# The state-space projection as seven products of tile sums, run between gate tiles that are moved there

## The chip, the core and the metric

The kernel runs on one core of a Trainium2 chip. A core has a matrix engine (TensorE, PE in the profile), VectorE (DVE), ScalarE (ACT), GpSimd (POOL) and SyncE (SP), which issues most of the weight loads. Each engine works through a queue of its own in order and waits on semaphores of the others. The metric is the device time of one execution in microseconds; the median of three runs before the change is 2598.36 (2598.11 to 2598.48).

## What is computed

One layer of a hybrid encoder over 384 tokens (256 of a prompt and 8 x 16 of running streams), all in float32. Cut to what matters:

```
proj = rmsnorm(x) @ w_in                      # pool | z | xBC | dt | gates, gates = 2 x 2048 columns
a_pool = pool_mixer(proj_pool)                # 384 x 2048
a_ssd  = gated_rmsnorm(ssd_scan(...), z)      # 384 x 4096
br_pool = a_pool @ w_pool_proj                # 2048 x 2048
br_ssd  = a_ssd  @ w_ssd_proj                 # 4096 x 2048   <- the state-space projection
merged = sigmoid(gate_A) * br_pool + sigmoid(gate_B) * br_ssd
x = x + rmsnorm(merged @ w_out)               # 2048 x 2048
x = x + rmsnorm(relu(rmsnorm(x) @ w_up)**2 @ w_down)
```

## The kernel before

Activations lie transposed in SBUF, channels on the 128 partitions and the 384 tokens along the row. To keep float32 precision at the speed of the float32r form, each operand is split in a high part (ACT copies it to float32r: `wh`, `xgh`) and a low part (DVE takes the difference: `wl`, `xgl`), and each product is three matmuls: high by high, high by low, low by high. A weight tile of 128 x 1024 (512 KB) is loaded by SP (`wfetch`), split by one ACT and one DVE instruction (`wsplit`) into pools of three buffers each, and then used by 24 matmuls of 384 columns (`half`) or, where tokens are stationary and the weights move, by 18 matmuls of 512 columns (`moving`).

The stages, in order of time in the profiled execution:

- up to 585 us: the norm, the pooling branch and its projection. `gate_a(i)` makes tile i of the first gate (product with `w_ga`, times `rstd`, sigmoid), `pool_out(i)` multiplies it with the pool product and stores it in DRAM as `ma_scr[i]`. All sixteen of them are made here, the last twelve in blocks of four ahead of the four `pool_out` that use them.
- to about 1150: the scan over eight groups; its result goes to DRAM as `a_scr[0..31]`, one tile of 128 channels each. Between and behind its last steps come the tiles of the second gate (`gate_b(i)`, stored as `gb_scr[i]`), 0 to 7. A list `queue` of weight loads runs three splits ahead of their use (`take`). The scan's last norm (`finish`, `store`) stands at 1184 on DVE, beside gate tiles 8 to 15, and POOL stores the four last `a_scr` tiles behind it.
- 1246 to 1496: the state-space projection, `pj_sp`: 16 output tiles, each 32 channel tiles x 3 matmuls of 384 columns, weights stationary. Behind each tile DVE multiplies with `gbr` (loaded from `gb_scr`), adds `mar` (loaded from `ma_scr`), and ACT and DVE split the sum into `mh` and `ml`, the left operands of the next product. `gbr` and `mar` have two buffers each and are loaded by POOL.
- to about 1620: the product with `w_out`, tokens stationary: four column blocks of 512, each eight weight tiles (units) of two channel tiles, into three PSUM banks, one for each block of 128 tokens.
- to 2596: the MLP. Its down projection already uses the scheme that the change brings to the state-space projection, and its names are the same: for token blocks 0 and 1, two halves of the channels and two column blocks of 512, the 2 x 2 block product is made with seven products of sums in place of eight (`b11, b21, U, b22, W, V, X`), four more make block 2 as before. Sums of the token tiles (slots 6 to 9 of ten) are made by DVE, sums of the weights by one load with addition on POOL (`accum_op`) and by three DVE additions (`AHEAD`). A product `m` has a PSUM bank that is filled from the accumulator `acc` by an ACT copy (a seed, `opened`) and copied back by ACT or added by DVE (`taken`). `converted` turns the nine accumulators into the six output blocks. The forms run as two behind each half tile of the up projection.

The order on each engine comes from a list scheduler, which places instructions by the order of the program and by when it takes them to be ready; the hardware then runs each queue as placed. PSUM has two banks for projections (`mmtile`) and six others (`sstile`).

Of the kernel before, what the change touches and what calls it, by code (L numbers as in the profile page):

```python
# [14 lines left out]
P = 128  # L15
# [18 lines left out]
def build(ctx, tc, io):  # L34
# [110 lines left out]
    def moving(o, units, lhs, tail, done, pool=None, own=0, hook=None, mid=None, held=None):  # L145
# [12 lines left out]
        for kp in range(n - tail):  # L158
            wh, wl = take(*units[kp])
            with behind(last[0] if chain[0] else None):  # L160
                for k2 in range(2):
                    for b in range(3):
                        mm(b, wh, wl, kp * 2 + k2, k2)
            if hook and kp in hook:
                hook[kp]()
        w = [wload(*units[kp]) for kp in range(n - tail, n - own)]
# [46 lines left out]
    a_scr = [dram.tile([P, T], F32, name=f"a_scr{i}") for i in range(32)]  # L213
    ma_scr = [dram.tile([P, T], F32, name=f"ma_scr{i}") for i in range(KD)]
# [15 lines left out]
    yx = small.tile([P, 56], F32, name="yx")[:, :3]  # L230
# [137 lines left out]
    tok = small.tile([P, 11, NH], F32, name="tok")  # L368
    decb = small.tile([P, NH, NB], F32, name="decb")
    with tc.tile_pool(name="phc", bufs=1, reuse_waits="tile") as pc, tc.tile_pool(name="phc2", bufs=2, reuse_waits="tile") as pc2:  # L370
# [94 lines left out]
        def pool_out(i, sg):  # L465
            ps = proj([io["w_pp"][i, q] for q in range(2)], A, f"pp{i}")
            v.tensor_tensor(halves(sg), even_odd(ps), halves(sg), ALU.mult)
            gp.dma_start(ma_scr[i], sg)
# [98 lines left out]
        for nb in range(4):  # L567
            if nb:
                sg = [gate_a(nb * 4 + i) for i in range(4)]
            for i in range(4):  # L570
                pool_out(nb * 4 + i, sg[i])
            if nb == 0:
                dt_turn(srcs)

    def gate_b(i, pool, tag, hook=None):
        ps = proj([io["w_gb"][i, q] for q in range(2)], xg, f"gb{i}", hook)
        t = pool.tile([P, T], F32, tag=tag, name=f"gbt{i}")
# [5 lines left out]
    with tc.tile_pool(name="phd", bufs=2, reuse_waits="tile") as pd, tc.tile_pool(  # L583
# [350 lines left out]
        queue.extend((io["w_gb"][i, q], f"gb{i}_{q}") for i in range(KD) for q in range(2))  # L934
        queue.extend((io["w_ssd"][i, q], f"sp{i}_{q}") for i in range(KD) for q in range(4))
        queue.extend((io["w_out"][nb, kp], f"wo{nb}_{kp}") for nb in range(4) for kp in range(8 if nb < 3 else 3))
# [146 lines left out]

    mpool = ExitStack()
    with ExitStack() as phe:
        pe1 = phe.enter_context(tc.tile_pool(name="phe", bufs=1, reuse_waits="tile"))
        pe2 = phe.enter_context(tc.tile_pool(name="phe2", bufs=4, reuse_waits="tile"))
        pe4 = phe.enter_context(tc.tile_pool(name="phe4", bufs=2, reuse_waits="tile"))
        ab = []

        def aload():
            for i in (len(ab), len(ab) + 1):
                a = pe2.tile([P, T], F32, tag="ar", name=f"ar{i}")
                sy.dma_start(a, a_scr[i])
                h = pe1.tile([P, T], F32R, name=f"abh{i}")
                l = pe1.tile([P, T], F32R, name=f"abl{i}")
                with later():
                    s.activation(h, a, AF.Copy)
                    v.tensor_tensor(l, a, h.bitcast(F32), ALU.subtract)
                ab.append((h, l))  # L1100

        for i in range(8, KD):
            gate_b(i, pe4, "gbt", aload)
        chain[0] = False
        main.close()
        mp = mpool.enter_context(tc.tile_pool(name="mp", bufs=1, side="right", reuse_waits="tile"))
        for i in range(KD):
            ma, gb = (mp.tile([P, T], F32, tag=f"{n}r", name=f"{n}r{i}", bufs=2) for n in ("ma", "gb"))
            gp.dma_start(ma, ma_scr[i])
            gp.dma_start(gb, gb_scr[i])  # L1110
            ps = proj([io["w_ssd"][i, q] for q in range(4)], ab, f"sp{i}")
            h = mp.tile([P, T], F32R, name=f"mh{i}")
            l = mp.tile([P, T], F32R, name=f"ml{i}")
            v.tensor_tensor(halves(gb), even_odd(ps), halves(gb), ALU.mult)
            v.tensor_tensor(ma, ma, gb, ALU.add)
            s.activation(h, ma, AF.Copy)
            v.tensor_tensor(l, ma, h.bitcast(F32), ALU.subtract)
            ms_.append((h, l))

    res = ctx.enter_context(tc.tile_pool(name="res", bufs=1, reuse_waits="tile"))  # L1120

    r2 = res.tile([P, T], F32, name="r2")
# [24 lines left out]
    for b in range(3):  # L1147
        sy.dma_start(x1[:, b, :], io["x_tok"][b])
    NE = 4
    upool = ExitStack()  # L1150
    pg0 = upool.enter_context(tc.tile_pool(name="pg0", bufs=1, reuse_waits="tile"))
# [7 lines left out]
    xtiles(pg0, NE)  # L1159
    with tc.tile_pool(name="phf", bufs=1, side="right", reuse_waits="tile") as pf, tc.tile_pool(  # L1160
# [80 lines left out]
        for nb in range(4):  # L1241
# [3 lines left out]
            o = [sstile(f"wo{nb}_{b}") for b in range(3)]  # L1245
# [4 lines left out]
            def done(b):  # L1250
# [22 lines left out]
                [(io["w_out"][nb, kp], f"wo{nb}_{kp}") for kp in range(8)],  # L1273
# [6 lines left out]
                {(2, 3): first_turns} if nb == 3 else None,  # L1280
            )
# [125 lines left out]
    with tc.tile_pool(name="phg", bufs=1, side="right", reuse_waits="tile") as pg, tc.tile_pool(  # L1407
# [3 lines left out]
        ORDER = ("b11", "b21", "U", "b22", "W", "V", "X")  # L1411
        AHEAD = {
            "U": ("W", "U", "U", "b22", ALU.add),
            "b22": ("V", "b11", "W", "b11", ALU.subtract),
            "W": ("X", "b21", "b21", "W", ALU.add),
        }
        USES = {
            "b11": ((0, 0), (7, 2)),
            "b21": ((1, 3), (7, 5)),
            "b22": ((2, 8), (8, 9)),  # L1420
            "X": ((3, 4),),
            "U": ((4, 6),),
            "W": ((5, 7),),
            "V": ((6, 1), (8, 2)),
        }
        SEEDED = (0, 1, 2, 3, 4, 5, 6)
        LEFT = {(0, 0): 1, (0, 1): 2, (1, 0): 3, (1, 1): 6, (2, 0): 7, (2, 1): 8}
        first = {m: f for f in reversed(ORDER) for m, _ in USES[f]}
        final = {m: f for f in ORDER for m, _ in USES[f]}
# [3 lines left out]
        def ff_tile(f8, ps, plain):  # L1433
# [16 lines left out]
            elif q:  # L1450
                x = V2[p]
                for o, a, b in ((6, 1, 4), (7, 0, 6), (8, 3, 7), (9, 5, 2), (1, 1, 0)):
                    v.tensor_tensor(x[:, o], x[:, a], x[:, b], ALU.subtract)
# [4 lines left out]
        hacc = lambda b, nb: acc[:, nb // 2 * 9 + LEFT[b, nb % 2], :]  # L1458

        def split(w, name):  # L1460
            h = wpool.tile([P, 1024], F32R, tag="wh", name=f"wh_{name}")
            l = wpool.tile([P, 1024], F32R, tag="wl", name=f"wl_{name}")
            s.activation(h, w, AF.Copy)
            v.tensor_tensor(l, w, h.bitcast(F32), ALU.subtract)
            return h, l

        def quad(G4, np_):
            c8, g = divmod(G4, 2)
            fh, fl = FH[g], FL[g]
            bank, kept = {}, {}  # L1470

            def load():
                for i, j in ((1, 2), (1, 1), (2, 1), (2, 2)):
                    w = pg.tile([P, 1024], F32, tag="wd", name=f"w_b{i}{j}_{G4}_{np_}", bufs=7)
                    sy.dma_start(w, io["w_down"][c8, np_ * 2 + j - 1, g * 2 + i - 1])
# [279 lines left out]
```

## Time and profile before

| what | number |
|---|---|
| median of three runs | 2598.36 us |
| profiled execution, its time | 2597.85 us |
| its span from first to last instruction | 2596.0 us |
| TensorE clock granted, mean | 0.999 |
| `pj_sp` stage | 1246.3 to 1495.7 us |
| `pj_ga` matmuls, all sixteen tiles | 768, 326 ns recorded each |

The page and its views are read like this: a busy time is the time in which an engine had an instruction under way; the chain that ended last follows the last instruction back to what released it; a row of the groups gives line, engine, operation, output and inputs, count, busy time and mean ns of one, and the idle time before them with what ended it; the timeline gives start, length and count. A row by stage has the length of the stretch, then for each engine its busy time and (x) instructions, then the granted clock, the share of time that the DMA engines were busy, and GB/s. The recorded length of a matmul overlaps that of the next, so its price in a stream is the distance from start to start.

### The profile page before, as it was taken

How to read it: one execution, taken by the hardware profiler on the slowest of the kernel's cores; microseconds unless marked ns; L12 is line 12 of the kernel's file. 1: busy time of each engine (PE TensorE's matmuls, PEld its weight loads, DVE VectorE, ACT ScalarE, POOL GpSimd, SP SyncE). 2: the span in 40 equal slices, each digit the busy share in tenths (PEclk: the TensorE clock that was granted, in tenths of full speed). 3: DMA queues.
4: the chain of work that ended last, by engine and by line, in shares of the span. 5: the costliest groups of instructions: out<-in, count | busy, mean ns of one | idle time of the engine just before them, and what ended most of it. 6: DMA issues, size and time to landing. Idle time of an engine off the chain costs nothing.

```text
span 2596.0 us, 41253 instructions
## 1 busy us (share of the span) xinstructions
PE 2586.1 (100%) x16021; PEld 2493.7 (96%) x16021; DVE 1798.9 (69%) x2553; ACT 1434.7 (55%) x2215; POOL 396.1 (15%) x579
## 2 busy tenths in 40 slices
PE   9999999999999999999999999999999999999998
PEld 9999999999999999999999988999999999999997
DVE  6676335789999999876444335767777777777766
ACT  6443333656566666655323334666676666666653
POOL 0000002254355444521000000000000000000000
PEclk9999999999999999999999999999999999999999
DMA  7444446666766676757544455555455554555434
GB/s 279 151 137 150 149 149 215 201 210 220 241 223 230 214 245 226 239 205 245 185 161 162 153 190 183 192 168 155 147 162 163 169 164 146 155 157 166 140 136 173
DMA packets 139158, 477.34 MB, mean 184 GB/s; under 512 B 21089, under 2 KB 28065, under 8 KB 133201
## 3 DMA queue, kind: packets, MB, share of 16 engines
q1 hardware_dynamic: 103552, 361.44, 41.9%
q0 software_dynamic: 28352, 98.45, 12.6%
q10 hardware_dynamic: 7056, 14.81, 1.8%
q8 instruction: 126, 2.06, 0.3%
q14 instruction: 72, 0.58, 0.1%
HBM read 427.10 MB, written 47.52 MB: 183 GB/s over the span
## 4 chain that ended last, share of the span: by engine, by line
PE 99%; ACT 0%; DVE 0%; DMA 0%; DVEq 0%; issue 0%
PE pj_up L101 6%; PE pj_up L103 6%; PE pj_up L102 6%; PE wd L1515 5%; PE wd L1516 5%; PE wd L1514 5%; PE pj_x L101 5%; PE pj_x L102 5%; PE pj_x L103 5%; PE pj_sp L102 3%; PE pj_z L103 3%; PE pj_z L101 3%; PE pj_sp L103 3%; PE pj_sp L101 3%; PE pj_z L102 3%; PE pj_gb L101 2%
## 5 line engine op out<-in xcount | busy, mean ns | idle before, releaser
L101 PE MATMUL pj_up<-x1h,wh_up 128*128 128x384 f32 (+1 forms) x1024 | 333.7, 326 | 0.0
L102 PE MATMUL pj_up<-x1l,wh_up 128*128 128x384 f32 (+1 forms) x1024 | 333.4, 326 | 0.0
L103 PE MATMUL pj_up<-x1h,wl_up 128*128 128x384 f32 (+1 forms) x1024 | 333.4, 326 | 0.0
L70 ACT ACTIVATE wh_up<-w_up 128x1024 fp32r<-128x1024 f32 x126 | 133.2, 1057 | 219.0 <-PE pj_up L102 205.7
L101 PE MATMUL pj_x<-xgh,wh_x 128*128 128x384 f32 x768 | 251.9, 328 | 0.0
L102 PE MATMUL pj_x<-xgl,wh_x 128*128 128x384 f32 x768 | 250.4, 326 | 0.0
L103 PE MATMUL pj_x<-xgh,wl_x 128*128 128x384 f32 x768 | 250.4, 326 | 0.0
L102 PEld LDWEIGHTS pj_up<-x1l,wh_up 128*128 128x128 f32 x1024 | 193.6, 189 | 2.6
L101 PEld LDWEIGHTS pj_up<-x1h,wh_up 128*128 128x128 f32 x1024 | 193.6, 189 | 2.6
L103 PEld LDWEIGHTS pj_up<-x1h,wl_up 128*128 128x128 f32 x1024 | 193.6, 189 | 0.0
L71 DVE TENSOR_TENSOR wl_up<-w_up,wh_up 128x1024 fp32r<-128x1024 f32 x126 | 154.1, 1223 | 56.5 <-ACT wh_up L70 56.4
L101 PE MATMUL pj_z<-xgh,wh_z 128*128 128x384 f32 x512 | 166.9, 326 | 0.0
L102 PE MATMUL pj_z<-xgl,wh_z 128*128 128x384 f32 x512 | 166.9, 326 | 0.0
L103 PE MATMUL pj_z<-xgh,wl_z 128*128 128x384 f32 x512 | 166.9, 326 | 0.0
L101 PE MATMUL pj_sp<-abh,wh_sp 128*128 128x384 f32 x512 | 166.9, 326 | 0.0
L102 PE MATMUL pj_sp<-abl,wh_sp 128*128 128x384 f32 x512 | 166.9, 326 | 0.0
L103 PE MATMUL pj_sp<-abh,wl_sp 128*128 128x384 f32 x512 | 166.9, 326 | 0.0
L70 ACT ACTIVATE wh_sp<-w_sp 128x1024 fp32r<-128x1024 f32 x64 | 67.8, 1059 | 166.3 <-PE pj_sp L102 158.2
L71 DVE TENSOR_TENSOR wl_sp<-w_sp,wh_sp 128x1024 fp32r<-128x1024 f32 x64 | 78.4, 1225 | 116.5 <-ACT wh_sp L70 116.5
L101 PEld LDWEIGHTS pj_x<-xgh,wh_x 128*128 128x128 f32 x768 | 145.1, 189 | 2.1 <-issue 0.4
L102 PEld LDWEIGHTS pj_x<-xgl,wh_x 128*128 128x128 f32 x768 | 145.2, 189 | 0.0
L103 PEld LDWEIGHTS pj_x<-xgh,wl_x 128*128 128x128 f32 x768 | 145.2, 189 | 0.0
(401 smaller groups left out, 7429.3 us busy)
## 6 DMA issues: line engine op xcount, KB each, us to landing
w_up<-w_up SPq DMA_DIRECT2D x128, 512.0 KB, 3.7
w_b<-w_down SPq DMA_DIRECT2D x112, 512.0 KB, 4.3
w_x<-w_in SPq DMA_DIRECT2D x96, 512.0 KB, 3.9
w_z<-w_in SPq DMA_DIRECT2D x64, 512.0 KB, 4.2
w_sp<-w_ssd SPq DMA_DIRECT2D x64, 512.0 KB, 3.4
w_ga<-w_ga SPq DMA_DIRECT2D x32, 512.0 KB, 3.5
w_pp<-w_pp SPq DMA_DIRECT2D x32, 512.0 KB, 3.4
hs<-ssm POOLq DMA_DIRECT2D x16, 1024.0 KB, 6.6
```

What stands on the lines that cost most here:

```text
L70: cut[0] = s.activation(h, w, AF.Copy)
L71: cut[1] = v.tensor_tensor(l, w, h.bitcast(F32), ALU.subtract)
L101: te.matmul(out, wh, xh, start=first, stop=False, **how)
L102: te.matmul(out, wh, xl, start=False, stop=False, **how)
L103: return te.matmul(out, wl, xh, start=False, stop=last, **how)
L1514: te.matmul(out, mh, vh, start=begin, stop=False, skip_group_check=held)
L1515: te.matmul(out, mh, vl, start=False, stop=False, skip_group_check=held)
L1516: te.matmul(out, ml, vh, start=False, stop=end, skip_group_check=held)
```

## The change

The product with `w_ssd_proj` is made as in the down projection: eight groups of four channel tiles (`gk`), two pairs of column blocks (`np_`), sixteen quads of seven forms. `w_ssd` is laid out for that by the host. The forms are not run in a stage of their own, but behind each half of 17 gate tiles: the twelve tiles of the first gate, 4 to 15, which leave the pooling stage (`gate_late`, with the pool product brought back from a new DRAM tile `pp_scr`), and tiles 8 to 12 of the second. Three or four forms follow each half, so that a quad (`b11 b21 U` | half | `b22 W V X` | half) goes with one gate tile. Since the sum now lies with tokens on the partitions, TensorE turns it back (`mt`, three transposes for each of 16 tiles) and `merge(n)` does what stood behind `pj_sp`: 0 to 3 in the last quad, 4 to 15 ahead of and between the units of the first column block of `w_out`.

```
+        def pool_out(i, sg):                      # nb > 0: no gate yet
+            if sg is None:
+                o = pc2.tile([P, T], F32, tag="sg", name=f"po{i}", bufs=5)
+                s.copy(halves(o), even_odd(ps))
+                gp.dma_start(pp_scr[i - 4], o)
+                return
...
+    def aload(gk):
+        x = pq.tile([P, 10, 2, P], F32, tag="ax", name=f"ax{gk}")
+        for q in range(2):
+            for p in range(2):
+                sy.dma_start(x[:, q * 3 : q * 3 + 3, p], a_scr[gk * 4 + q * 2 + p].rearrange("p (s t) -> p s t", s=3))
...
+    def diffs(gk):
+        x = raw[gk]
+        for o, a, b in DIFFS:
+            v.tensor_tensor(x[:, o], x[:, a], x[:, b], ALU.subtract)
+
+    def refill(gk, key):
...
+        s.activation(h, src, AF.Copy)
+        v.tensor_tensor(l, src, h.bitcast(F32), ALU.subtract)
...
+    def merge(n):
...
+        gp.dma_start(gb, gb_scr[n])
+        gp.dma_start(ma, ma_scr[n])
+        o = sstile(f"mt{n}")[:, :T]
+        for b in range(3):
+            te.transpose(o[:, b * P : b * P + P], hacc(acc, b, n // 4)[:, n % 4 * P : n % 4 * P + P], ident)
+        v.tensor_tensor(gb, o, gb, ALU.mult)
+        v.tensor_tensor(ma, ma, gb, ALU.add)
+        s.activation(h, ma, AF.Copy)
+        v.tensor_tensor(l, ma, h.bitcast(F32), ALU.subtract)
+
+    def gate_late(i, hook):
+        ps = proj([io["w_ga"][i, q] for q in range(2)], xg, f"ga{i}", hook)
+        t = pq.tile([P, T], F32, tag="gt", name=f"gat{i}", bufs=2)
+        pp = pq.tile([P, T], F32, tag="pt", name=f"ppt{i}")
+        gp.dma_start(pp, pp_scr[i - 4])
+        with later():
+            v.tensor_tensor(halves(t), even_odd(ps), halves(rstd), ALU.mult)
+            s.activation(t, t, AF.Sigmoid)
+            v.tensor_tensor(t, t, pp, ALU.mult)
+        gp.dma_start(ma_scr[i], t)
...
+        want = max(0, 112 * (done_[0] - 2) // (NH_ - 2))
+        forms(want - done_[1])
+        done_[1] = want
+
+    for i in range(4, KD):
+        gate_late(i, hook)
+    for i in range(8, 13):
+        gate_b(i, pq, "gt", hook, 2)
...
+    moving(o_first, wo_units(0), ms_, 0, None, None, 0, {i: merges(6 + 2 * i, 7 + 2 * i) for i in range(5)}, lo=0, hi=5)
...
-        sy.dma_start(x1[:, b, :], io["x_tok"][b])
+        gp.dma_start(x1[:, b, :], io["x_tok"][b])
```

`refill` makes the high and low part of the slots that one form uses (`ah...`, `al...`, one buffer each, two for one of them); the slots of group gk + 1 are refilled while group gk runs. The functions of the down projection (`quad`, `forms`, `converted`) are the same as before, moved up and shared.

Three places of the new order matter. On DVE, where the mixed stage begins: `zs` is the last step of the scan's norm, `gat` gate tile 4, `ax` the four channel tiles of group 0 with their sums, `al...` the low parts, and the last row the low split of the first form's weights.

```order
L925 SCALAR_TENSOR_TENSOR zs_3_11577<-zs_3_11577,vec,ny_g_12299 128x384
L1311 TENSOR_TENSOR gat_12436<-pj_ga_12338,rstd 128x384
L1313 TENSOR_TENSOR gat_12436<-gat_12436,ppt_12437 128x384
L1243 TENSOR_TENSOR alb_12375<-ax_12333,ahb_12374 128x256
L1243 TENSOR_TENSOR als_12379<-ax_12333,ahs_12378 128x256
L1235 TENSOR_TENSOR ax_12333<-ax_12333 128x256 x5
...
L1243 TENSOR_TENSOR alX_12433<-ax_12333,ahX_12432 128x256
L1121 TENSOR_TENSOR wl_b_sq_0_12486<-w_b_sq_0_12479,wh_b_sq_0_12485 128x1024
```

All of it stands behind the norm; on TensorE the first form follows gate tile 4 and the first half of tile 5. The second place is ACT in a middle quad, from the split of V's weights to that of the next gate half (`wh_ga`); `sq<-acs` is a seed, `acs<-sq` a copy back.

```order
L1120 ACTIVATE wh_V_sq_1_13691<-w_b_sq_1_13550 128x1024
L1312 ACTIVATE gat_13733<-gat_13733 128x384
L1141 COPY sq_1_6_13678<-acs 128x512
L1146 COPY acs<-sq_1_2_13600 128x512
L1141 COPY sq_1_3_13695<-acs 128x512
L1120 ACTIVATE wh_X_sq_1_13715<-w_b_sq_1_13552 128x1024
L1141 COPY sq_0_0_13719<-acs 128x512
L1146 COPY acs<-sq_1_5_13650 128x512
L1242 ACTIVATE ahb_13729<-ax_13490 128x512
L70 ACTIVATE wh_ga_0_13743<-w_ga_0_13741 128x1024
```

Before, the gate halves' splits had no seeds or copies back between them. The third is POOL where the merges go on: `gb_scr_147` is the store of the last gate tile, `gbr` and `mar` are the loads of merges 4, 5 and 6.

```order
L1295 DMA gbr_16171<-gb_scr_136 128x384
L1296 DMA mar_16170<-ma_scr_120 128x384
L589 DMA gb_scr_147<-gbt_16158 128x384
L1295 DMA gbr_16185<-gb_scr_137 128x384
L1296 DMA mar_16184<-ma_scr_121 128x384
L1295 DMA gbr_16223<-gb_scr_138 128x384
L1296 DMA mar_16222<-ma_scr_122 128x384
```

Only the first pair of loads is ahead of the last gate tile's store; before, each such pair stood behind the product of the tile two before it.

More of the change, by code (lines that the diff above doesn't have):

```diff
@@ L1082, in build @@
     ms_ = []
[L1084 to L1118, printed above, removed]
@@ L1457, in build, with wd_quad @@
         acc = pg.tile([P, 18, 512], F32, name="acc")
[L1458 to L1467, printed above, removed]
+        def wd_quad(G4, np_):
             c8, g = divmod(G4, 2)
```

350 lines of the change are left out of this document (232 added, 118 removed).

## The prediction

> **What bounds the kernel now.** I read the busy shares and the chain of waits first, then the list of what TensorE (PE) waited for, then a table by stage.
>
> ```profile
> PE 2586.1 (100%) x16021; PEld 2493.7 (96%) x16021; DVE 1798.9 (69%) x2553; ACT 1434.7 (55%) x2215; POOL 396.1 (15%) x579
> PE 99%; ACT 0%; DVE 0%; DMA 0%; DVEq 0%; issue 0%
> ...
> PE warm_o L246 <- DVE warm L242: 1.2, 1, 1.2
> PE pj_p L322 <- ACT xgh L282: 0.2, 1, 0.2
> ...
> core 0: us, PE busy (x) PEld busy (x) DVE busy (x) ACT busy (x) POOL busy (x), PEclk, DMA share, GB/s
> 330.00:585.00 255.00, 255.00 (x1705) 252.34 (x1704) 164.01 (x228) 124.95 (x210) 69.64 (x113) 1.00 0.60 195
> 585.00:1158.00 573.00, 573.00 (x4386) 559.74 (x4385) 517.50 (x791) 363.54 (x674) 257.86 (x350) 1.00 0.68 227
> 1246.00:1496.00 250.00, 250.00 (x1540) 250.00 (x1539) 101.47 (x110) 76.13 (x81) 16.67 (x31) 1.00 0.49 160
> 1720.00:2480.00 760.00, 760.00 (x4128) 714.92 (x4127) 549.17 (x660) 524.07 (x717) 20.71 (x24) 1.00 0.51 155
> ```
>
> PE is the whole chain, and it waits 1.4 us in the 2596.0 us span. So every matmul taken away shortens the time, and every wait that PE gains lengthens it. The stage that is rebuilt (1246 to 1496) has VectorE (DVE) busy 41% and ScalarE (ACT) 30%: there is room. In the down projection (1720 to 2480), which already uses seven products, DVE stands at 72% and ACT at 69%, still without a PE wait.
>
> **The products.** A matmul's recorded length overlaps the next one's, so the cost of one is the distance between starts.
>
> ```profile
> L101 PE MATMUL pj_sp<-abh,wh_sp x512: 326/326/326, 1246.3 to 1495.4; 128*128 128x384 f32 x171
> L103 PE MATMUL pj_sp<-abh,wl_sp x512: 326/326/326, 1246.6 to 1495.7; 128*128 128x384 f32 x171
> ...
> 1989.31 0.38 PE L1514 MATMUL wd<-wh_X,fh 128*128 128x512 f32 x1
> ...
> 1993.19 0.33 PE L101 MATMUL pj_up<-x1h,wh_up 128*128 128x384 f32 x1
> ...
> 1617.61 1.04 PE L1198 MATMUL trm<-cst,x 128*128 128x128 f32 x8
> 1618.40 0.46 PE L154 MATMUL wo<-eh_wo,mh 128*128 128x512 f32 x1
> 1618.70 0.38 PE L155 MATMUL wo<-el_wo,mh 128*128 128x512 f32 x1
> ```
>
> Before: 3 x 512 matmuls of 384 columns from 1246.3 to 1495.7, 0.1625 us each, 249.6 us. Now: 16 quads of 11 uses x 2 x 3 = 1056 matmuls of 512 columns. Between 1989.31 and 1993.19 stand 18 of them, 0.2156 each, so 227.7 us: **-21.9**. The sum is transposed back in 16 groups of three. Eight transposes took 0.79 us, three 0.30, and the matmul behind takes 0.30 where 0.216 is usual: 0.38 x 16 = **+6.1**. The twelve gate tiles keep their matmuls: 0. Where they stood, twelve copies of 384 columns by ACT and twelve stores take their place: nothing, since ACT is busy 125 of 255 us there (330 to 585) and PE 255; uncovered they would be some 6 us. The 64 weight loads stay on SP; the 16 accumulating ones on POOL (8 MB more) lie in a stage whose DMA share was 0.49. PE's own work falls by 15.8 us; the rest is what it comes to wait for.
>
> **Entry to the mixed stage.** The last norm of the scan (at 1184.2 here) is DVE work that until now lay beside eight gate tiles with weights split three ahead. Now the first sums of the seven products stand behind it on DVE, in the order shown with the change.
>
> ```profile
> 1184.23 0.55 DVE L208 TENSOR_SCALAR ssum<-bc_g 128x384 f32<-128x384 f32 x1
> ...
> 1192.96 2.20 DVE L917 SCALAR_TENSOR_TENSOR zs<-zs,vec,ny_g 128x384 f32<-128x384 f32 x4
> 1195.07 1.22 DVE L71 TENSOR_TENSOR wl_gb<-w_gb,wh_gb 128x1024 fp32r<-128x1024 f32 x1
> ...
> 1193.87 2.14 POOL L920 DMA_DIRECT2D a_scr<-zs  x4 [7.92 <-DVE zs L917]
> ...
> DMA to landing us min/median/max: 2.6/2.7/4.5
> ...
> DMA to landing us min/median/max: 3.3/3.8/4.8
> ...
> L900 DVE TENSOR_TENSOR xs<-xs,Yb 128x256 f32<-128x256 f32 x32 | 13.1, 415 | 0.0
> L1493 DVE TENSOR_TENSOR acc<-wd,acc 128x512 f32<-128x512 f32 x52 | 35.6, 684 | 0.0
> L1464 DVE TENSOR_TENSOR wl_b<-w_b,wh_b 128x1024 fp32r<-128x1024 f32 x84 | 102.7, 1223 | 26.5 <-ACT wh_b L1463 26.4
> L1501 DVE TENSOR_TENSOR w_b<-w_b,w_b 128x1024 f32<-128x1024 f32 x84 | 101.6, 1222 | 1.4
> w_b<-w_down POOLq DMA_DIRECT2D x28, 512.0 KB, 8.3
> ```
>
> PE starts gate tile 4 at 1184.2 and has 72 matmuls (11.7 us) before form b11: it is there at 1195.9. DVE ends the norm's four zs rows about 1.6 us sooner than now (a split and a gate product are no longer between), at 1193.6. POOL issues four stores behind them, then the load of the pool product ppt, at 1194.4 (1193.87 + 2.14 - 1.6); loads of that size (gbr and mar, the two landing lines) need 2.7 and 3.8 us: 1197.1 to 1198.2. The gate's last product (0.56) waits for it, and all below is in order behind: low parts and differences of group 0 (eleven rows of 256 columns, two of 512: 4.6 + 1.4 us), then b11's low split, 1.2. PE starts at about 1205.4: **9.5 us of wait**. Next, U's accumulating load stands behind that gate's store on POOL (8.3 us to land, 1207.5), just in time; but behind U's split two sums of weights, two short rows and the split of the gate half (4.5 us) leave PE waiting 1 to 3 more. Entry: **+11**, from 8 (load at its fastest, rows overlapping by a tenth) to 14.
>
> **Inside the mix.** A quad is b11, b21, U, gate half H1, b22, W, V, X, gate half H2: 66 x 0.2156 + 48 x 0.1625 = 22.0 us of PE.
>
> ```profile
> L1463 ACT ACTIVATE wh_b<-w_b 128x1024 fp32r<-128x1024 f32 x84 | 89.1, 1060 | 30.1 <-PE pj_up L102 14.2 <-ACT acc L1491 12.8 <-PE wd L1516 3.0
> L1486 ACT COPY wd<-acc 128x512 f32<-128x512 f32 x182 | 104.4, 592 | 0.0
> L1491 ACT COPY acc<-wd 128x512 f32<-128x512 f32 x200 | 116.6, 583 | 23.0 <-PE wd L1516 22.9
> L1445 ACT ACTIVATE ff<-ff 128x384 f32<-128x384 f32 x64 | 32.8, 512 | 1.5 <-DVE ff L1442 1.5
> L816 ACT ACTIVATE xhl<-xT 128x512 fp32r<-128x512 f32 x16 | 10.0, 625 | 4.7 <-DVE xT L802 4.7
> ```
>
> Two quads cost ACT 18 splits (19.1), 28 copies to and from the banks (16.5), 7 high parts (two of 512 columns, five of half that: 3) and 2 sigmoids (1): 39.6 of 44 us, 90%. DVE has 18 splits (22.0), 6 sums of weights (7.3), 4 additions (2.7), differences and low parts (5.5) and 4 gate rows (2.2): 39.7. Weights have three buffers, so the tight place is H2: its split may begin only when W is through (3.9 us before H2's turn), and on ACT it stands behind sigmoid, three seeds, two takes and X's split, that could not begin before H1's tile was done, 7.8 us before H2's turn. With some 1.6 us for H1's tail on DVE: 1.6 + 0.5 + 3 x 0.59 + 2 x 0.58 + 1.06 = 6.1, then 1.06 and 1.22 for H2's own halves: 8.4 against 7.8, and 0.6 more in each second quad, where b22's high part stands between. Rows in a run start somewhat before the record of the one ahead ends (1192.96 + 2.20 is four rows of 0.61), which takes up to 0.6 off again. So 0 to 1.2 late; I take 0.5 in 14 seeded quads, **+7**, between 0 and 14. In the last two quads DVE loses the 5.5 us of refills and gets fourteen conversions of 512 columns (9.6) and four merges of three rows (6.7): 50.5 us against 44. The 6.5 too many end partly behind the quads, beside gate tiles 14 and 15: **+3**, 0 to 6.
>
> **Merges into the output projection.** Merges 4 to 15 now run beside the first column block of w_out: a pair for each 18 matmuls (3.9 us and the transposes). Before, a merge had 15.6 us.
>
> ```profile
> 1263.53 0.54 POOL L1110 DMA_DIRECT2D gbr<-gb_scr  x1 [13.79 <-DVE mar L1115]
> 1265.13 0.54 POOL L1109 DMA_DIRECT2D mar<-ma_scr  x1 [1.07 <-DVE ml L1117]
> ...
> L1115 DVE TENSOR_TENSOR mar<-mar,gbr x16: 559/560/560, 1262.7 to 1496.7; 128x384 f32<-128x384 f32 x16
> ```
>
> A buffer of mar is loaded again 2.4 us after its addition begins (1262.7 to 1265.13), and lands 3.8 later: 6.2 us a round for two merges, where PE needs 4.3 a pair. POOL holds the second pair's loads behind the store of gate 15, so there is no lead. From the third unit on PE loses up to 1.9 per pair, five times, 9.5; a little less where rounds overlap: **+8**, 4 to 11. Loads of x_tok, 1 MB each, stand on the same queue ahead of the last pair.
>
> The sum: -21.9 + 6.1 + 11 + 7 + 3 + 8 = +13.2. The profiled execution took 2597.85 (span 2596.0, 1.85 around it), 0.5 under the median of 2598.36: forecast **2611**.
>
> **The clock.** After a long wait PE may also run slower.
>
> ```profile
> 2577.00:2596.00 19.00, 10.59 (x50) 8.92 (x48) 13.96 (x30) 3.02 (x9) 0.00 (x0) 0.92 0.44 167
> ...
> 4.16 0.69 PE L322 MATMUL pj_p<-xgh,wh_e 128*128 128x384 f32 x1 [0.23 <-ACT xgh L282]
> ...
> 10.69 0.33 PE L101 MATMUL pj_p<-xgh,wh_e 128*128 128x384 f32 x1
> ```
>
> Where PE lies idle 8.4 us at the end, the granted clock averages 0.92. The first 24 products from 4.16 to 10.69 took 6.5 us, 2.6 more than at 0.1625, waits included: that is the most a cold restart costs by rows. The Trainium skill, TensorE: Matmul & The Clock Gate, section HAM oscillation, says that an idle gap of over about 3.4 us halves the clock until PE has been busy again; by it the entry gap alone would add an estimated 2 us. The fall of the clock in the last window agrees with it.
>
> **The rivals.** (1) Faster, 0.24: the splits run far enough ahead. Three weight buffers and two banks for gate tiles hold 4 to 8 us of PE's work, and the stage from 585 to 1158 shows that this can do: DVE is busy 517.5 of its 573 us, 90% as in the mix, and PE never waits. Then quads and merges cost nothing and the entry some 5, where ppt and the refills come sooner: -15.8 + 5 gives 2588. Against it: the norm and the refill are one in-order run of DVE rows. It decides when all waits together stay under 10.6 us. (2) Same, 0.12: entry and merges at their low ends (8 + 4) with 4 in the mix and the last quad: 2598. (3) ACT becomes the bound in the mix: every quad at 1.0 late, a cold restart at the entry and merges at 11: -15.8 + 14 + 14 + 6 + 11 + 2.6 = 2630, 0.12. (4) The seven products save PE nothing, because a form costs more in the mix than the 0.2156 it takes in the down projection: then the 21.9 us are missing, 2633, 0.02.
>
> **Numbers.** The forecast has 0.50; with rivals 3 and 4 slower holds 0.64, faster 0.24, same 0.12. About 0.2% (5.2 us) can be told from no change. The forecast's own range is 2600 to 2624 (terms at half way to their ends); for 8 in 10 it must take in most of rival 2 and part of rival 1, so 2590 to 2624.
>
> **What would show it.** A PE wait of 7 us or more at the first form behind a DVE split; short waits at H2 once a quad; PE waits in the first block of w_out for ml; sq products at 0.2156. Wrong if PE shows under 10 us of waits in all, or if a queue (SP's weights or POOL's accumulating loads) ends most of them.

## The result, and the profile after

The changed kernel takes 2614.62 us (median of 4 runs, 2613.52 to 2616.11), the kernel before 2598.24 on the same chip: 1.0064 times as long, 95% interval 1.0046 to 1.0081. The forecast was 2611, range 2590 to 2624, slower with 0.64. The profiled execution's span went from 2596.0 to 2612.7 us.

Two starts split these 16.7 us. The rows are from the timelines of PE, first before, then after: the first product of w_out and the first of w_up (start, length, engine, line, operation).

```profile
1495.88 0.38 PE L154 MATMUL wo<-wh_wo,mh 128*128 128x512 f32 x1
...
1622.30 0.36 PE L101 MATMUL pj_up<-x1h,wh_up 128*128 128x256 f32 x1
```

```profile
1494.79 0.38 PE L154 MATMUL wo<-wh_wo,mh 128*128 128x512 f32 x1
...
1638.96 0.36 PE L101 MATMUL pj_up<-x1h,wh_up 128*128 128x256 f32 x1
```

Up to w_out the change is 1.1 us ahead. In the output projection it loses 17.7 (144.2 us against 126.4), and from w_up to the last product nothing moves any more. The list of PE's waits after names the places (line of the waiting group, what it waited for: total us, times, longest):

```profile
PE sq L1169 <- ACT wh_b_sq L1120: 11.3, 1, 11.3
PE mt L1299 <- DVE gbr L1300: 4.4, 5, 1.6
PE wo L154 <- ACT mh L1302: 3.8, 1, 3.8
PE pj_gb L103 <- DVE wl_gb L71: 1.4, 1, 1.4
...
PE sq L1170 <- DVE wl_b_sq L1121: 0.9, 1, 0.9
PE pj_gb L101 <- ACT wh_gb L70: 0.7, 1, 0.7
```

They sum to 22.5 us. The waits alone don't make the time, since the clock falls behind them. The table by stretch of five us (PE busy, its weight loads, DVE, ACT and POOL, granted clock, DMA share, GB/s) shows it at the entry and in the merges:

```profile
1105.00:1110.00 5.00, 0.00 (x0) 0.00 (x0) 0.52 (x2) 0.00 (x0) 0.00 (x0) 0.59 0.59 234
1110.00:1115.00 5.00, 0.95 (x2) 0.50 (x2) 5.00 (x15) 3.87 (x7) 1.99 (x3) 0.50 0.57 122
1115.00:1120.00 5.00, 4.15 (x11) 3.19 (x11) 3.68 (x5) 1.95 (x3) 0.00 (x0) 0.55 0.97 237
1120.00:1125.00 5.00, 5.00 (x26) 4.49 (x26) 4.96 (x6) 3.81 (x6) 0.11 (x1) 1.00 0.83 294
...
1510.00:1515.00 5.00, 3.39 (x12) 2.73 (x13) 3.40 (x7) 2.00 (x3) 2.03 (x4) 0.70 0.81 262
...
1535.00:1540.00 5.00, 2.55 (x6) 2.10 (x7) 3.68 (x6) 1.89 (x3) 0.00 (x0) 0.59 0.98 389
```

To price each place I took, from the timeline of PE, the distance from one matmul's start to the next and subtracted 0.1625 us (384 columns) or 0.2156 (512). What is left over, place by place (slow clock is what products lose at 0.43 us apart; the rest is waiting):

| place | predicted | measured | of it slow clock |
|---|---|---|---|
| products, 1536 of 384 to 1056 of 512 columns | -21.9 | -21.9 | |
| 48 transposes | +6.1 | +5.9 | |
| entry to the mixed stage | +11 (8 to 14) | +14.8 | 2.4 |
| inside the mix, 16 quads | +7 (0 to 14) | +0.5 | |
| last two quads, gate tile 12 | +3 (0 to 6) | +2.7 | |
| merges beside w_out's first block | +8 (4 to 11) | +13.9 | 4.3 |
| sum | +13.2 | +15.9 (16.7 by the spans) | 6.7 |

**The entry.** The timeline of POOL and DVE around it:

```profile
1099.51 2.14 POOL L928 DMA_DIRECT2D a_scr<-zs  x4 [6.56 <-DVE zs L925]
...
1101.64 0.54 POOL L1309 DMA_DIRECT2D ppt<-pp_scr  x1
...
1109.48 0.56 DVE L1313 TENSOR_TENSOR gat<-gat,ppt 128x384 f32<-128x384 f32 x1 [8.21 <-DMA ppt<-pp_scr]
```

The product with ppt stands where the prediction put it, ahead of every low part, and DVE waits for the load there. But 7.8 us lie between the load's issue and that product (1101.64 to 1109.48), not 2.7 to 3.8. PE's last gate matmul starts at 1102.41, the first form at 1114.05:

```profile
1102.41 0.33 PE L103 MATMUL pj_ga<-xgh,wl_ga 128*128 128x384 f32 x1
1114.05 0.80 PE L1169 MATMUL sq<-wh_b_sq,ahb 128*128 128x512 f32 x1 [11.31 <-ACT wh_b_sq L1120]
...
1117.14 0.63 PE L1169 MATMUL sq<-wh_b_sq,ahb 128*128 128x512 f32 x1
1117.57 0.63 PE L1170 MATMUL sq<-wl_b_sq,ahb 128*128 128x512 f32 x1
```

Behind the gap the products start 0.43 us apart (1117.14, 1117.57), twice the usual, until 1119.4.

**Inside the mix.** The tight place is H2, the second gate half of a quad. One of them, ACT and DVE rows ahead of PE's arrival:

```profile
1217.57 0.53 ACT L1312 ACTIVATE gat<-gat 128x384 f32<-128x384 f32 x1 [0.39 <-DVE gat L1311]
...
1218.00 0.58 ACT L1141 COPY sq<-acs 128x512 f32<-128x512 f32 x1
...
1222.56 1.23 DVE L71 TENSOR_TENSOR wl_ga<-w_ga,wh_ga 128x1024 fp32r<-128x1024 f32 x1 [0.73 <-ACT wh_ga L70]
...
1223.86 0.33 PE L101 MATMUL pj_ga<-xgh,wh_ga 128*128 128x384 f32 x1
```

The low part ends at 1223.79, 7.7 us after H1's last matmul (1215.92 to 1216.09) and 0.07 before PE's turn: neither late nor early. The order is the predicted one (sigmoid, seed, take, seed, split X, seed, take, split), only each row starts 0.1 us before the record of the one ahead ends (1217.57 + 0.53 is 1218.10, the next starts at 1218.00). Seven such steps are the 0.7 between the predicted 8.4 and this.

**The merges.** The last pair, on POOL, DVE and PE:

```profile
1525.92 0.54 POOL L1386 DMA_DIRECT2D x<-x_tok  x1
...
1530.51 0.54 POOL L1295 DMA_DIRECT2D gbr<-gb_scr  x1 [0.52 <-DVE mar L1301]
...
1535.81 0.56 DVE L1300 TENSOR_TENSOR gbr<-mt,gbr 128x384 f32<-128x384 f32 x1 [1.43 <-DMA gbr<-gb_scr]
...
1537.45 0.79 PE L154 MATMUL wo<-wh_wo,mh 128*128 128x512 f32 x1 [3.82 <-ACT mh L1302]
```

The load waits for its buffer (idle 0.52 behind the addition of an earlier merge), is issued at 1530.51 behind 1 MB of x_tok, and lands 5.3 us later. PE stands 3.8 us and then runs 5 us at half clock.

### The profile page after: what moved, and what is told of

It is laid out like the page before. It is cut to its first block, busy times and chain, and to the rows that moved or that the text cites. A ratio compares the mean times of both kernels' runs of the same rounds, so it can differ in the third digit from the quotient of the medians.

```text
span 2612.7 us, 41084 instructions
## 1 busy us (share of the span) xinstructions
PE 2580.1 (99%) x15589; PEld 2452.8 (94%) x15589; DVE 1955.3 (75%) x2763; ACT 1597.7 (61%) x2520; POOL 425.4 (16%) x622
## 4 chain that ended last, share of the span: by engine, by line
PE 95%; issue 2%; DVE 1%; DMA 1%; POOL 1%; ACT 0%; DVEq 0%; POOLq 0%; ACTq 0%
PE pj_up L101 6%; PE pj_up L103 6%; PE pj_up L102 6%; PE wd L1170 5%; PE wd L1169 5%; PE wd L1171 5%; PE pj_x L101 5%; PE pj_x L102 5%; PE pj_x L103 5%; PE pj_z L103 3%; PE pj_z L102 3%; PE pj_z L101 3%; PE sq L1170 3%; PE sq L1171 3%; PE sq L1169 3%
## 5 line engine op out<-in xcount | busy, mean ns | idle before, releaser
L1133 POOL DMA_DIRECT2D w_b_wd<-w_down x28 | 24.2, 865 | 773.2 <-DMA w_b_wd<-w_down 742.5
L71 DVE TENSOR_TENSOR wl_x<-w_x,wh_x 128x1024 fp32r<-128x1024 f32 x96 | 116.8, 1221 | 30.1 <-ACT wh_x L70 30.1
L70 ACT ACTIVATE wh_x<-w_x 128x1024 fp32r<-128x1024 f32 x96 | 100.3, 1052 | 59.9 <-PE pj_z L102 30.9
L1146 ACT COPY acc<-wd 128x512 f32<-128x512 f32 x200 | 116.5, 583 | 23.0 <-PE wd L1171 22.9
L1169 PE MATMUL wd<-wh_b_wd,fh 128*128 128x512 f32 x336 | 127.3, 379 | 0.0
```

The lines of the kernel that those rows point to most:

```text
L70: cut[0] = s.activation(h, w, AF.Copy)
L71: cut[1] = v.tensor_tensor(l, w, h.bitcast(F32), ALU.subtract)
L1133: gp.dma_start(w, unit(0, np_ * 2), accum_op=ALU.add)
L1146: s.copy(dst, o)
L1169: te.matmul(out, mh, vh, start=begin, stop=False, skip_group_check=held)
```

## The experiments

Ten kernels, in the order in which they ran. Unless said otherwise each is the changed kernel with one edit; all times are medians, beside 2614.62 for the change and 2597.8 to 2598.2 for the kernel before.

### 1. The forms begin two halves later

```diff
-    NH_ = 34
+    NH_ = 36
-        want = max(0, 112 * (done_[0] - 2) // (NH_ - 2))
+        want = max(0, 112 * (done_[0] - 4) // (NH_ - 4))
-    for i in range(8, 13):
+    for i in range(8, 14):
...
```

> The forms begin two weight halves later (at the fifth half instead of the third) and end two later, inside gate tile 13; their density stays 3.5 a half. Theory: the wait at the first form is a fixed lateness of the first sums behind the last norm and the pool product's load, so 48 more gate matmuls (48 x 0.1625 = 7.8 us) cover 7.8 of its 11.65 us, and the slow clock behind it gets shorter or goes: a wait of 3 to 5 us at the first form, 8 to 10 us less in all, 2605 to 2607, unless the end of the mix, which now has only gate tiles 14 and 15 behind it, gives back up to 4. Rival (the entry is bound by throughput of DVE and DMA in that stretch, not by one late chain): the wait moves to the new first form nearly whole, 8 us or more, and the time stays within 3 us of 2614.6.

Measured: 2610.06 (1.0047, 1.0032 to 1.0062), 4.6 less, half of what was expected. The wait at the first form fell from 11.3 to 4.3 us (and 1.0 more behind it), as the theory has it: the first form starts at 1114.35, where it started at 1114.05 before, with 48 more gate matmuls ahead of it. So the lateness can be covered. That it is one fixed lateness is not shown, since another chain ends in the first form here: the loads of the first sums (`ax`) are issued from 1102.88 on, in the change from 1093.40, and ACT waits for them until 1108.73. The pool product's load, still on POOL's queue behind the four stores, is much less late. Two lists of DMA issues show it, first the change, 1098 to 1102, then this kernel, 1099.9 to 1102.4 (issuing queue, count, KB each, median us to landing):

```profile
w_b_sq<-w_ssd SPq DMA_DIRECT2D x4, 512.0 KB, 6.8
a_scr<-zs POOLq DMA_DIRECT2D x4, 192.0 KB, 7.1
ppt<-pp_scr POOLq DMA_DIRECT2D x1, 192.0 KB, 7.7
```

```profile
a_scr<-zs POOLq DMA_DIRECT2D x4, 192.0 KB, 2.4
ppt<-pp_scr POOLq DMA_DIRECT2D x1, 192.0 KB, 4.4
```

In the change SP issues the first quad's four weight blocks from 1098.06 to 1100.42, just ahead of stores and load; here it issues them from 1105.56 on, behind them. So it is these blocks, more than the place on POOL's queue, that make the load late.

At the entry 6.2 us are gained (8.7 over the plain distances, 14.9 before). The clock falls behind 4.3 us of waiting as it did behind 11.3: a dozen products in a row are 0.43 apart. And 1.7 us are lost again at the end of the mix: the two waits of 0.7 and 1.4 us for gate weights halve the clock in this run (1473.4 to 1476.8), which they did not in the change.

### 2. Four buffers for the merges' loads

```diff
-            ma, gb = (mp.tile([P, T], F32, tag=f"{a}r", name=f"{a}r{n}", bufs=2) for a in ("ma", "gb"))
+            ma, gb = (mp.tile([P, T], F32, tag=f"{a}r", name=f"{a}r{n}", bufs=4) for a in ("ma", "gb"))
```

> Four buffers each for the merges' two loads instead of two. Theory: the two-buffer round of a load (it is issued only when the rows of the merge before last are through) sets the pace of merges 8 to 15; with four, loads lie two pairs ahead: the five waits of 0.8 to 1.6 us for gbr and the slow clock behind them go (5.5 + 1.7), and the last pair's wait of 3.8 with its 2.6 us of slow clock goes too, since the x_tok loads now stand behind all merges on the queue: 2602 to 2608. Rival (DVE, with the splits of w_out between the merge rows, or the transfers themselves set the pace): the waits stay, 2612 to 2616.

Measured: 2608.94 (1.0042, 1.0027 to 1.0057), 5.7 less, 1 us above the expected range. The two waits of the merges fell from 4.4 and 3.8 to 1.0 and nothing, so the two-buffer round was the pace. (The wait at the first form, which the edit does not touch, came out at 12.1 in this run, 0.8 more.) A new wait took the last one's place; in the list of PE's waits of this kernel:

```profile
PE wo L154 <- ACT wh_wo L70: 2.7, 1, 2.7
...
PE mt L1299 <- DVE gbr L1300: 1.0, 1, 1.0
...
PE wo L155 <- DVE wl_wo L71: 0.5, 1, 0.5
```

and the table by stretch says why: all three x_tok loads now stand in one run behind the merges, and the DMA engines are full when the weights of w_out are due.

```profile
1525.00:1530.00 5.00, 5.00 (x25) 4.38 (x24) 0.52 (x2) 0.00 (x0) 0.00 (x0) 1.00 1.03 423
1530.00:1535.00 5.00, 1.88 (x6) 0.94 (x5) 1.64 (x2) 3.22 (x6) 0.00 (x0) 0.81 0.52 208
```

### 3. The first pool product's load on another queue

```diff
-        gp.dma_start(pp, pp_scr[i - 4])
+        (s if i == 4 else gp).dma_start(pp, pp_scr[i - 4])
```

> The first pool product's load (gate tile 4) goes on ACT's DMA queue instead of POOL's, where it stands behind the four stores of the last norm. Theory: the load takes 7.8 us because it is queued behind these stores; on another queue it has landed before the gate's product wants it, DVE's run of low parts begins at about 1102 instead of 1109.5, the first form's wait falls from 11.3 to 3 to 5 us, and with the slow clock behind it 7 to 9 us are gained: 2605 to 2608. Rival (the 16 DMA engines are full there, 0.93 busy, or DVE's own rows are what is late): 2 us or less.

Measured: 2612.6 (1.0055, 1.004 to 1.007), 2.0 less: the rival's number. The load is issued at 1090.80, 11 us earlier and so ahead of stores and weight blocks alike, and the gate's product runs at 1101.32 without waiting, so the first half of the theory holds. The second half does not: the first form starts at 1110.42, 3.6 earlier, not 7. Its timeline shows what is late next:

```profile
1101.32 0.56 DVE L1313 TENSOR_TENSOR gat<-gat,ppt 128x384 f32<-128x384 f32 x1 [0.59 <-ACT gat L1312]
...
1107.72 0.42 ACT L1242 ACTIVATE ahW<-ax 128x256 fp32r<-128x256 f32 x1 [4.09 <-DMA a_scr<-zs]
```

ACT's high part of slot W is held until a store of the last norm has landed. The two share no data; that its memory is taken over from the stored tile is an inference, which no run here tests. The stores, issued from 1098.96 on beside the weight blocks, land that late while the DMA engines are full:

```profile
1100.00:1105.00 5.00, 2.19 (x14) 1.90 (x12) 4.41 (x12) 2.38 (x6) 3.09 (x6) 1.00 0.90 274
1105.00:1110.00 5.00, 0.00 (x0) 0.00 (x0) 0.71 (x2) 1.93 (x4) 0.00 (x0) 0.65 1.04 365
```

The Trainium skill, DMA: Bandwidth & Descriptors, section Queues, rings and completion order, says that the queues of SP and ACT are rings on the same 16 DMA engines; by it another queue is a way past what is queued, but no more bandwidth. That is what the run shows: the load no longer waits, and the stretch is no emptier (share 0.90 and 1.04, in the change 0.93 and 0.59). At the entry 2.7 us are gained; 1.5 of them are lost again where the waits of 0.7 and 1.4 us for gate weights halve the clock, as in experiment 1. The total alone would have hidden both.

### 4. One more copy in each quad

```diff
-                        s.copy(bank[m], acc[:, np_ * 9 + m, :])
+                        [s.copy(bank[m], acc[:, np_ * 9 + m, :]) for _ in range(1 + (m == 3 and nm[:2] == 'sq'))]
```

> One more copy of 512 columns on ACT (0.58 us) in each of the 14 seeded quads: the bank that form X opens is seeded twice. Nothing else is changed. Theory: the low part of the second gate half's weights is done 0.07 us before PE wants it (1223.79 against 1223.86), so the mix has no slack there, though ACT is busy only 36 of 44 us: each seeded quad loses about 0.5, 7 us in all, 2620 to 2623, seen as gaps at the second gate half. Rival (weights split three ahead hide a copy): the time stays within 2 us of 2614.6.

Measured: 2623.49 (1.0099, 1.0082 to 1.0116), 8.9 more, a little over the theory's 2620 to 2623. Two quads took 44.17 us from one H2 to the same row two quads later; now 45.21 (1225.42 to 1270.63), some 0.4 us of it at H2 and 0.6 at the b11 behind the next gate half. Inside the mix this comes to 6.3 us, a little under the theory's 7. The rest of the 8.9 lies elsewhere: the waits of 0.7 and 1.4 us at gate tile 12 halve the clock in this run (1479.6 to 1483.0, 1.7 us), and the entry is 1.1 longer. So an ACT that is busy 36 of 44 us has no room for 0.58 us at this place: the order of its rows, not its load, is the limit.

### 5. Four buffers, and x_tok between the weights

On top of experiment 2:

```diff
-    for b in range(3):
-        gp.dma_start(x1[:, b, :], io["x_tok"][b])
...
+            if nb < 3:
+                sy.dma_start(x1[:, nb, :], io["x_tok"][nb])
```

> Four merge buffers as before, and the three loads of x_tok (1 MB each), which stood in one run on POOL's queue behind the merges, go on SP, one by one between the weights of the second block of w_out. Theory: with four buffers alone the last wait moved to the weights of w_out (2.7 + 0.5 us and a slow clock of some 3), because 3 MB of x_tok land there at once (DMA share 1.03, 423 GB/s from 1525 to 1530); spread out, this goes: 2602 to 2604. Rival (the merges' own loads fill the queues there, or SP is late for another reason): 2607 to 2610, the wait for the split of w_out's weights stays over 2 us.

Measured: 2603.54 (1.0021, 1.0012 to 1.0031), as the theory has it. Of the merges one wait of 1.1 us is left, and the clock of the whole stretch (1497 to 1557) is 1.00, where the change had 0.91 (1495 to 1555). With experiment 2 this is nearly the whole price of the merges: by the same distances 13.1 of the 13.9 us are gone there. The time falls by 11.1 only; the wait at the first form is 12.4 in this run, 1.1 more than in the change.

### 6. No mixing

```diff
-        want = max(0, 112 * (done_[0] - 2) // (NH_ - 2))
+        want = 112 * (done_[0] // NH_)
```

> All 112 forms run in one piece behind gate tile 12's last half, none between the gate halves. Everything else is as in the change. Theory: without gate matmuls between them two quads give PE 28.5 us, and ACT and DVE need some 30.5 each (35.9 and 37.5 in 44 us, less four splits and two gate tails): PE waits at least 2 us in each two quads and, since the runs of splits are in order, up to 6: 16 to 48 us more; the entry costs nothing now (11 + 3 less): 2617 to 2650. Rival (the mixing buys nothing, forms alone keep PE busy): 2600 or less.

Measured: 2629.62 (1.0121, 1.0106 to 1.0136), 15.0 more than the change, inside the theory's range. Among its waits there are now fifteen for the weights of forms X and W:

```profile
PE sq L1169 <- ACT wh_X_sq L1120: 5.3, 10, 0.8
...
PE sq L1169 <- ACT wh_W_sq L1120: 2.8, 5, 0.8
```

Four quads take 62.55 us (1330.14 to 1392.69, the same row of form X), 31.3 for two; their products alone are 28.5. Eight times the difference, about 22 us, is the work of ACT and DVE that mixing hides behind gate matmuls. The entry gives back about half of that: it costs 14.8 us in the change and 4.3 here (one wait of 2.4 and the slow clock behind it).

### 7. Matmuls that nobody reads, in the gap

```diff
+        if done_[0] == 3:
+            wt = sstile("fill")
+            for _ in range(60):
+                te.matmul(wt[:, :T], xg[0][0][:, :P], xg[0][0], start=True, stop=True)
```

> 60 matmuls of 384 columns, whose product nobody reads, stand on PE ahead of the first form (9.75 us at 0.1625), in the gap of 11.65 us. Nothing else is changed. Theory: the form's products behind the gap took 0.43 instead of 0.2156 apart for 5 us because PE had stood still; kept busy, it runs at full clock from the first one: granted clock 1.00 from 1114 on, 1.5 to 3 us less (the low part of the first weights still comes 2 us behind the first product): 2611 to 2613. Rival (the forms' products are slow there for another reason, their operands or the full DMA engines): products 0.43 apart as before, 2614 to 2616.

Measured: 2616.03 (1.007, 1.0053 to 1.0087): no gain, the theory's 2611 to 2613 is missed. Its table by single us (PE busy, clock, DMA share, GB/s) tells why:

```profile
1113.00:1114.00 1.00, 0.15 (x1) 1.00 0.65 142
1114.00:1115.00 1.00, 0.48 (x1) 1.00 0.84 119
1115.00:1116.00 1.00, 0.00 (x0) 1.00 1.02 197
1116.00:1117.00 1.00, 0.63 (x3) 1.00 0.93 185
1117.00:1118.00 1.00, 1.00 (x6) 0.77 1.05 300
1118.00:1119.00 1.00, 1.00 (x4) 0.50 0.89 246
```

The clock is whole at the first form now, so the standing still does set it. But two waits are left, of 1.15 and 1.59 us with one product between them; from 1113 to 1117 PE is busy 1.26 us, and 1.2 us after the second wait the clock is halved all the same, for 3.4 us. The low part of the first weights is ready no earlier than in the change (its first product starts at 1116.37, there at 1116.12), and 1.7 us more are lost to the clock behind the waits of 0.7 and 1.4 us at gate tile 12. The theory's cause stands; that filling most of the gap removes it does not.

### 8. All repairs together

Experiment 3's and 5's edits, and forms from the seventh half on, to gate tile 14:

```diff
-    NH_ = 34
+    NH_ = 38
-        want = max(0, 112 * (done_[0] - 2) // (NH_ - 2))
+        want = min(112, max(0, 112 * (done_[0] - 6) // (NH_ - 6)))
-    for i in range(8, 13):
+    for i in range(8, 15):
...
```

> Forms begin four halves later and reach to gate tile 14, the first pool product's load is on ACT's queue, four merge buffers, x_tok between the weights of w_out's second block. Theory: the first sums are ready at about 1114 whatever PE does; four halves are 15.6 us of cover for a wait of 11.65, so the entry costs nothing and no slow clock follows; merges cost 1 to 2; the last quad's 2.7 stay; net work -15.8: 2584 to 2589. Rival (the waits move on: the entry to the new first form, the end of the mix to the one gate tile that is left behind it, where conversions and merges 4 and 5 are late): 2592 to 2602.

Measured: 2592.83 (0.9979, 0.997 to 0.9989): 0.2% faster than the kernel before, a small difference but clear of the interval, and in the rival's range. The waits moved on. In its list:

```profile
PE pj_ga L103 <- DVE wl_ga L71: 2.9, 2, 1.9
PE sq L1170 <- DVE wl_U_sq L1121: 2.8, 1, 2.8
```

The first form waits no more; the gate halves ahead of and behind it and form U do.

### 9. The first quad's weights with the first sums

```diff
-            if f == ORDER[0]:
+            if f == ORDER[0] and not kept:
                 load()
...
+        if nm == "sq0_0":
+            load()
```

on top of experiment 8.

> As the kernel with all repairs, and the four weight blocks of the first quad, with the one that is accumulated on POOL, are issued together with the first sums instead of with form b11. Theory: in that kernel form U's low part was 2.8 us late because its accumulating load came late, behind the second gate product on POOL; issued earlier the wait of 2.8 and the 0.6 of slow clock behind it go, the 1.9 and 1.0 us for gate weights stay: 2588 to 2590.5. Rival (DVE's run of low parts, not the load, is what is late): the wait stays, 2592 to 2594.

Measured: 2591.59 (0.9979, 0.997 to 0.9989), the same ratio as experiment 8, so no gain that can be told: neither the theory's range nor the rival's. The edit moved little. The four blocks are issued from 1105.25 on, in experiment 8 from 1105.50, and the accumulating load at 1111.60 instead of 1113.05, since POOL waits there until the block that it adds to has landed. U's wait did fall, from 2.8 to 1.1, but gate weights took it up (3.5 where it was 2.9). From 1105 to 1130 the DMA engines are full in every five us:

```profile
1105.00:1110.00 5.00, 5.00 (x32) 5.00 (x32) 2.32 (x6) 2.21 (x5) 1.07 (x2) 1.00 1.05 341
1110.00:1115.00 5.00, 3.93 (x25) 3.64 (x23) 5.00 (x12) 3.75 (x8) 1.40 (x2) 1.00 1.02 410
```

and DVE and ACT, in order, wait for what lands late (2.65 us for the third pool product, 4.1 for the next group's sums). Forms begun later only meet the same transfers later.

### 10. Eight halves ahead of the forms

As experiment 9, with 8 in place of 6 in both places of `want`.

> As the one before, and the forms begin two halves later still, in 30 halves instead of 32: 3.73 forms a half. Theory (the entry is a fixed lateness): all three waits at the entry go, 2585 to 2588. Rival (the denser mix has no slack, since one more copy of 0.58 us a quad already cost 9 us): the second gate half's weights come late in most quads, 0.3 to 0.6 us each, 2590 to 2597.

Measured: 2600.24 (1.0009, 1.0000 to 1.0018), above both ranges: more cover at the start costs 8.7 us. The entry keeps 1.8 and 0.8 us of waits, so it is not one fixed lateness any more; and 3.73 forms a half leave less room everywhere else:

```profile
PE pj_gb L103 <- DVE wl_gb L71: 2.8, 1, 2.8
...
PE sq L1170 <- DVE wl_b_sq L1121: 1.9, 1, 1.9
PE wo L154 <- ACT wh_wo L70: 1.4, 1, 1.4
```

The first and the last are the end of the mix, where the last quads' conversions meet it. The loss is a few waits of 1.4 to 2.8 us, with 3.4 us of slow clock behind two of them, not 0.3 to 0.6 in most quads, as the rival had it.

## Why the prediction was right, and where it was not

**What bounds the kernel.** PE did, before and after; every us of the difference is a wait of PE, a slow stretch behind one, or work it was given or spared. That part needs no change.

**Products and transposes.** The products are right: 36 of the mix from 1127.83 to 1135.60 are 0.216 apart. Rival 4 (they save nothing) is out. The transposes are right or a little high: a group of three that nothing delays costs 0.32 us (1461.90 to 1462.44, less one product), 5.2 for sixteen; the 5.9 of the table has small waits beside them in it.

**Entry, +11, measured 14.8.** The chain was right: the norm, the pool product's load, the refill in order on DVE, then the form. One link was another: the first product waits for the high part of its weights, which stands behind ACT's own rows of the refill, and DVE's low split adds only 0.9. The term that was mis-sized is the load, 2.7 to 3.8 us in the prediction, taken from landings in a stage with a DMA share of 0.49, 7.8 in fact. The prediction moved the loads but did not ask what else is in flight there: the first quad's four blocks and the stores of the norm come at the same time, share 0.93 from 1100 to 1105, and where the blocks come behind it (experiment 1) the same load takes 4.4. Part of the error was given back, since from the gate's product to the first form it took 4.6 us (1109.48 to 1114.05; 6.6 to the first product with the low part) where the prediction added up 7.8. The second step, 1 to 3 us of waits at the gate half behind form U, did not come; PE, at half clock, came later itself.

**Inside the mix, +7, measured 0.5.** The place was right and shown by experiment 4, the size not: 8.4 us for H2's chain is a sum of recorded lengths, and rows that follow each other start 0.1 earlier. The prediction named this overlap ("takes up to 0.6 off again") and then still took 0.5 late; at zero slack that is the whole term. Its sign, short waits at H2 once a quad, did not show, and rival 3 (ACT bounds the mix) is out with it.

**Last quads, +3, measured 2.7.** Two waits for gate weights at gate tile 12, behind the conversions and merges on DVE and ACT.

**Merges, +8, measured 13.9.** The waits are 9.6 and the round of two buffers is their cause (experiment 2); 1 MB of x_tok, which the prediction only mentioned, stands ahead of the last load in the longest of them; no run separates the two there, since experiment 2 moved both. In experiment 2 PE then comes to wait behind the x_tok loads, as experiment 5 shows. The other 4.3 are slow clock.

**The clock, left out of the sum, 6.7 us.** The prediction priced it by rows at the entry only, 2.6 us at most, and kept it for a rival; it did not think of it in the merges. The Trainium skill, TensorE: Matmul & The Clock Gate, section HAM oscillation, warns of gaps over about 3.4 us; by it the 3.8 us of the last pair cost clock too, and the trace agrees. Waits of 1.6 and 0.9 us with three transposes between them did it as well.

So 2611 came out 3.6 us from the truth because a term that was too high by 6.5 and a term that was missing, 6.7, nearly cancel: that the number is so near is luck, that the change is slower is not. Of the rivals, the first (2588, splits run ahead) was right about the mix and wrong about the rest: its condition, all waits under 10.6 us together, is what experiments 8 and 9 came near, with 10.8 and 9.4 us of losses left (2592.83 and 2591.59 are 5.0 and 6.4 under the kernel before in their rounds, where the work saved is 15.8).

What stays open: how short the entry can be. In experiments 1 and 8 to 10 the pool product's load is no longer what is latest, but then the loads of the sums and of the weights are, with a DMA share of 1.0; no run took transfers away altogether.

## What to carry to other kernels

A change that spares the bounding engine work must be priced at its seams: here 16 us of PE work were spared, the steady mix cost half a us, and the entry, the last quads and the merges gave back 31. At a seam, list every transfer that is in flight there and not only the ones you add, above all the large ones that are issued just ahead of it. A wait of PE cost its length plus up to some 3 us of slow clock behind it here, so cover it whole or leave it short, and before moving work earlier or later look at what stands at zero slack in between: one copy of 0.58 us in a quad, in an engine with a fifth of its time free, cost 6 us there.

## What had not been expected of the hardware

The clock does not go by the length of one wait. It was halved behind single waits of 11.3, 4.3, 3.8 and 2.8 us, and behind pairs of 1.6 + 0.9 us (the change, 1508.7 to 1512.1), 1.15 + 1.59 (experiment 7) and 1.1 + 2.0 (experiment 9, from 1124.3). It was not behind 2.1 + 0.9 in experiment 3, where PE was busy only 1.0 us of the four from 1507 to 1511. And waits of the same length did both: a single one of 1.9 us halved it in experiment 10 (ending at 1356.8) and not in experiment 8 (ending at 1116.1); the pair of 0.7 + 1.4 for gate weights did not in the change (1468.4 to 1471.9), in experiments 2 and 5, and did in experiments 1, 3, 4 and 7.

What differs is when the wait comes. In the change the clock falls or rises at 1105.86, 1119.51, 1512.05, 1515.46, 1535.94 and 1542.77 (the clock column by single us gives them: 0.93 from 1105 to 1106 is a fall at 1105.86). The distances, 13.65, 392.53, 3.41, 20.48 and 6.83 us, are 4, 115, 1, 6 and 2 times 3.413. In each of the ten other profiles, too, all such distances are whole multiples of it, so a slow stretch is 3.41 us long or a multiple of that. The Trainium skill, TensorE: Matmul & The Clock Gate, section What's actually happening, says that activity is watched in a window of some 3.4 us that runs freely; by it a pair of short waits counts or not as it falls in the window. The runs agree with that, and in experiment 7, too, the clock fell after PE was back at work. How much of a window must be idle they do not settle. For a reader of experiments it means that 1.5 to 2 us of a difference can be the place of the window alone.

A load of 192 KB on POOL's queue (`ppt`) took from 2.7 to 8.3 us to land in one and the same kernel, the change. The DMA share does not tell which is slow: the 8.3 us lie in a stretch with 0.78 and 208 GB/s (1135 to 1144), 4.7 in one with 0.92 and 230 GB/s (1197 to 1202). What was issued just ahead does: between 1134 and 1137 a 512 KB load by SP, one by POOL, a 192 KB store and this load follow each other and take 7.9, 8.5, 8.5 and 8.3 us; the load of 2.7 us was issued at 1110.87, when nothing had moved since 1109.
